# A two-layer hybrid mixer: gates and a product moved ahead of the recurrence's levels, and two roots taken as powers

## The chip, the core and the metric

The kernel runs on one core of one Trainium2 chip, in one launch. Its time is the device time of a run, in microseconds; three runs of the kernel before gave 2448.23, 2448.4 and 2450.8, a median of 2448.4. TensorE is called PE here, VectorE DVE, ScalarE ACT, GpSimd POOL, and SyncE (which issues the loads of the weights) SP.

## The reference

The program is two blocks one behind the other on 256 positions of width 1024. The change is in the second, in its hybrid mixer, once in each of two layers. From one projection `h @ w_in` a layer makes three mixers and joins them in one output product:

```python
proj = h @ w_in                               # qa ka va | qd kd vd | qh fh ih gh
z     = q_a @ k_a.T / 8                       # stick-breaking, 4 heads of 64, causal
log_w = log_sigmoid(z) + tail                 # tail: sum of log_sigmoid(-z) to the right
o_a   = exp(log_w) @ v_a
o_d   = dilated_mixture(rope(rms(qd)), rope(rms(kd)), vd)
log_f = logaddexp(log(lb), log1p(-lb) + log_sigmoid(fh))   # recurrence, 4 heads of 128
scores[t, s] = sum_d q_h[t, d] * k_h[s, d] * exp(g[t, d] - g[s, d])   # g = cumsum(log_f), s <= t
o_h   = rms(scores @ ih (+ the state of earlier chunks)) * gain * silu(gh)
y     = concat(o_a, o_d, o_h) @ w_out
x     = x + g2 * y
```

Everything is float32.

## The kernel before

A product with a weight matrix is three matmuls in a rounded format, hi*hi, lo*hi and hi*lo (`mm3`, L135 to L139). The weights come in 1 MB slots (128 x 2048, `load`); `split_w` (L113 to L131) cuts a slot into four pieces, for each of which ACT writes the high half (L125) and DVE the low half (L128), out of a pool of eight pieces each. `dense_A` makes 128 rows x 512 columns of a product, `dense_B` the transposed form. Results go to PSUM tiles of two tags with four buffers each, `w` and `acc`.

One layer of `hybrid` goes through these steps, in the order of the program before:

1. Products for the dilated attention, its roots (`rsqrt` at site 'd', L1185), rotation (L1186 to L1200), transposes (L1206), scores (L1219), softmax, transposes (L1243) and output (L1251).
2. Products for the recurrence: queries (L1263), forget gates (L1268), logarithm (L1273), running sums `G` by a scan on DVE (L1278).
3. Products `qa`, `ka`, `va` of the stick-breaking mixer (L1284 to L1288).
4. The recurrence's scores: the diagonal (L1300, L1304), then seven levels n = 0 to 6 (L1305 to L1335). A level takes differences of `G` on POOL (L1317, L1318), the exponential on ACT (L1319), two multiplications on DVE (L1320, L1321), eight matmuls with 64 columns on PE (L1328) and a masked copy into `ST` on DVE (L1331). The tile `E` of a level has three buffers, so level n + 3 waits for the matmuls of level n.
5. Stick-breaking: scores z (L1346, L1350), scaled by six operations on DVE (L1354 to L1356); Abs, Exp, Ln on ACT (L1358 to L1360) and their sum on DVE (L1361); tails on PE (L1366 to L1370); the weights' exponential (L1372); output (L1379, L1382).
6. The output gates: product 3072 with Sigmoid (L1393) and two multiplications (L1394, L1396); then the recurrence's values, product 2560 (`ih`, L1401).
7. The recurrence's output, half by half t = 0, 1: matmuls (L1421, L1422), Square (L1427), sum (L1429), root (`rsqrt` at site 'o', L1430), two multiplications (L1431, L1432), transposes (L1435), copies into `yT`.
8. The gate row (L1083) and the output product `y @ w_out` in four quarters: halves of the inner dimension (k0 = 0, 4) by halves of the columns (n = 0, 1); the quarters with k0 = 0 need only the two attention mixers.

The program is not run in this order. A scheduler of the language puts the instructions of each engine in an order when the kernel is built, by its own estimate of times and by the place in the program; on the chip each engine takes its instructions in that fixed order and waits where an input isn't there. So a step that is moved in the text changes the order of many others.

`root` (L171 to L189) forms a power -1/2. At the sites named in `PW` it is one POOL instruction with `ALU.pow` (L175); at the others it is a Newton iteration of twelve small operations on DVE (L179 to L188).

Of the kernel before, what the change touches and what calls it, by code (L numbers as in the profile page):

```python
# [11 lines left out]
F32 = mybir.dt.float32  # L12
# [8 lines left out]
P = 128  # L21
D = 1024
S = 256
# [17 lines left out]
def kernel(ctx: ExitStack, tc: tile.TileContext, A: dict, out: bass.AP, phases=None):  # L41
# [128 lines left out]
    PW = 'bqvwt'  # L170
# [979 lines left out]
    def hybrid(l, tables):  # L1150
# [3 lines left out]
        with tc.tile_pool(name=f"hyb{l}", bufs=1, reuse_waits="tile") as wk:  # L1154
# [134 lines left out]

            ST = t4("ST")  # L1290
# [45 lines left out]
            def parts6(v):  # L1336
                return v[:, :1024].rearrange("p (h t) -> p h t", h=4), v[:, 1024:].rearrange("p (h t) -> p h t", h=4)

            zm = m6()
            z0, z1 = parts6(zm)  # L1340
            p0 = [ps("acc").rearrange("p (i t) -> p i t", i=2) for _ in range(2)]
            p1 = [ps("acc")[:, :S].rearrange("p (i t) -> p i t", i=2) for _ in range(2)]
            for i in range(2):
                for j in range(2):
                    r = slice(64 * j, 64 * j + 64)
                    PE.matmul(p0[j][:, i], ka[r, i, :P], qa[r, i], start=True, stop=True, skip_group_check=True)  # L1346
            for i in range(2):
                for j in range(2):
                    r = slice(64 * j, 64 * j + 64)
                    PE.matmul(p1[j][:, i], ka[r, i, P:], qa[r, i, P:], start=True, stop=True, skip_group_check=True)  # L1350
            neg = sbneg[:, None, :].to_broadcast([P, 2, P])
            for j in range(2):
                hs = slice(2 * j, 2 * j + 2)
                V.scalar_tensor_tensor(z0[:, hs, :P], p0[j][:, :, :P], 0.125, neg, ALU.mult, ALU.add)  # L1354
                V.tensor_scalar(z0[:, hs, P:], p0[j][:, :, P:], 0.125, None, ALU.mult)
                V.scalar_tensor_tensor(z1[:, hs], p1[j], 0.125, neg, ALU.mult, ALU.add)  # L1356
            sp = m6()
            ACT.activation(sp, zm, AF.Abs)  # L1358
            ACT.activation(sp, sp, AF.Exp, scale=-1.0)
            ACT.activation(sp, sp, AF.Ln, bias=1.0)  # L1360
            V.scalar_tensor_tensor(sp, zm, 0.0, sp, ALU.max, ALU.add)  # L1361
            s0, s1 = parts6(sp)
            for b in range(2):
                pt = ps("acc").rearrange("p (i t) -> p i t", i=2)
                hs = slice(2 * b, 2 * b + 2)
                PE.matmul(pt, tri, s0[:, hs], start=True, stop=False, skip_group_check=True)  # L1366
                PE.matmul(pt[:, :, P:], ones, s1[:, hs], start=False, stop=True, skip_group_check=True)
                V.tensor_tensor(z0[:, hs], z0[:, hs], pt, ALU.subtract)
            pt = ps("acc")
            PE.matmul(pt, tri, sp[:, 1024:], start=True, stop=True)  # L1370
            V.tensor_tensor(zm[:, 1024:], zm[:, 1024:], pt, ALU.subtract)
            ACT.activation(zm, zm, AF.Exp)  # L1372
            pt = ps("acc").rearrange("p (i t) -> p i t", i=2)
            for i in range(2):
                for j in range(2):
                    r = slice(64 * j, 64 * j + 64)
                    hd = 2 * i + j
                    vs = slice(64 * hd, 64 * hd + 64)
                    PE.matmul(  # L1379
                        pt[r, i], va[:, 0, vs], z0[:, 2 * j + i], start=i == 0, stop=False, skip_group_check=True  # L1380
                    )
                    PE.matmul(  # L1382
                        pt[r, i, P:], va[:, 1, vs], z1[:, 2 * j + i], start=False, stop=True, skip_group_check=True
                    )
            for i in range(2):
                put_T(yT[0][:, i], yT[1][:, i], pt[:, i])

            mod_cols(l, 2)
            gh = t4("h4", bufs=3).rearrange("p a b -> p (a b)").rearrange("p (t n) -> p t n", t=2)
            g128 = bcast_row(wk, A["hgrn_norm_g_2"][l], P, "g128")  # L1390
            po = dense_A(h, w, 3072, 512)
            for t in range(2):
                ACT.activation(gh[:, t], po[t], AF.Sigmoid)  # L1393
                V.tensor_tensor(gh[:, t], gh[:, t], po[t], ALU.mult)  # L1394
                ghv = gh[:, t].rearrange("p (h v) -> p h v", h=4)
                V.tensor_tensor(ghv, ghv, g128[:, None, :].to_broadcast([P, 4, P]), ALU.mult)  # L1396
# [45 lines left out]
            for k0 in (0, 4):  # L1442
                for n in range(2):
                    dense_A(yT, A["w_out_2"][l], 512 * n, 512, k0, 4, po[2 * n : 2 * n + 2], (0, 7))
                    if k0 == 4:
                        for t in range(2):
                            add_gated(wk, po[2 * n + t], g, t, n)
# [188 lines left out]
```

## Time and profile before

| | |
|---|---|
| median of three runs | 2448.4 us |
| the profiled execution, its own time | 2449.72 us |
| its span in the profile | 2447.9 us |
| busy: PE, DVE, ACT, POOL | 88%, 50%, 40%, 13% |
| loads by SP's queue | 715.70 MB, 74.9% of the 16 engines' time |
| mean granted clock of PE | 0.927 |

The span is cut in 40 slices of 61 us each on the page. The first mixer of the change lies from 1531 to 1688 us, in slices 26 to 28; the second from 2088 to 2245 us, in slices 35 to 37. A granted clock of 1.00 is PE's upper level (2.4 GHz), 0.50 the lower (1.2 GHz).

### The profile page before, as it was taken

To read this page: it belongs to the slowest core of one execution; us is meant where nothing else is said; L and a number is where in the kernel's file an instruction comes from. 1 tells how busy PE (TensorE), PEld (TensorE's weight loads), DVE (VectorE), ACT (ScalarE), POOL (GpSimd) and SP (SyncE) were. 2 spreads that over 40 slices of the span, in tenths; PEclk is the share of its full clock that TensorE was granted. 3 is DMA by queue.
4 is the path that set the end of the run, shared out by engine and by line. 5 is a ranking of instruction groups with operands and counts; after the bars stand their busy time and mean duration, and the time that the engine had idled before them with its cause. 6 is when DMAs were issued, how large, how long until landed. Compare 5 with 4: busy or idle time off the path is not lost.

```text
span 2447.9 us, 38767 instructions
## 1 busy us (share of the span) xinstructions
PE 2147.4 (88%) x15680; PEld 1591.2 (65%) x15680; DVE 1230.1 (50%) x2277; ACT 979.2 (40%) x1834; POOL 315.3 (13%) x198
## 2 busy tenths in 40 slices
PE   8998867787689987677666999989999999999999
PEld 7887424443257843222113999877998999887998
DVE  6765101000048631000003996878986986878655
ACT  6653110000036510000003774656765775557553
POOL 2000000000000000000000650031640550030100
PEclk9999979888889998878778999999999999989999
DMA  7377999999983899999997885625875785624652
GB/s 301 128 301 318 418 420 419 420 420 420 420 339 104 327 383 419 419 420 420 420 420 299 326 302 193 222 69 187 320 278 185 288 308 195 221 87 146 234 188 87
DMA packets 100211, 721.35 MB, mean 295 GB/s; under 512 B 11470, under 2 KB 11598, under 8 KB 12992
## 3 DMA queue, kind: packets, MB, share of 16 engines
q1 hardware_dynamic: 98640, 715.70, 74.9%
q0 software_dynamic: 1104, 3.06, 0.5%
q8 instruction: 123, 2.02, 0.3%
q14 instruction: 56, 0.46, 0.0%
q10 hardware_dynamic: 288, 0.12, 0.0%
HBM read 717.78 MB, written 1.05 MB: 294 GB/s over the span
## 4 chain that ended last, share of the span: by engine, by line
PE 59%; DMA 31%; DVE 5%; ACT 2%; issue 2%; POOL 0%; SPq 0%; DVEq 0%; POOLq 0%; ACTq 0%
PE w L139 12%; PE w L138 12%; PE w L137 12%; DMA slot<-in_w_down_dram 9%; DMA slot<-in_w_up_dram 8%; DMA slot<-in_w_gate_dram 8%; DMA slot<-in_xattn_w_kv_dram 4%; PE acc L137 3%; PE acc L138 3%; PE acc L139 3%; PE w L958 2%; PE w L819 1%; PE w L993 1%; PE acc L1328 1%; PE acc L434 1%
## 5 line engine op out<-in xcount | busy, mean ns | idle before, releaser
L128 DVE TENSOR_TENSOR wl<-slot,wh 128x512 fp32r<-128x512 f32 x854 | 695.8, 844 | 222.4 <-ACT wh L125 218.4
L125 ACT ACTIVATE wh<-slot 128x512 fp32r<-128x512 f32 x856 | 522.7, 627 | 311.9 <-PE w L139 165.7
L137 PE MATMUL w<-hTh,wh 128*128 128x256 f32 x1792 | 511.6, 286 | 8.1 <-ACT hTh L356 6.1
L138 PE MATMUL w<-hTh,wl 128*128 128x256 f32 x1792 | 511.1, 285 | 3.2 <-DVE wl L128 3.2
L139 PE MATMUL w<-hTl,wh 128*128 128x256 f32 x1792 | 511.3, 285 | 0.0
L958 PE MATMUL w<-slot,XgT 128*32 128x256 f32 x4096 | 316.6, 445 | 126.6 <-DMA slot<-in_w_up_dram 93.7
L137 PEld LDWEIGHTS w<-hTh,wh 128*128 128x128 f32 x1792 | 346.4, 193 | 13.1 <-ACT hTh L356 7.0
L138 PEld LDWEIGHTS w<-hTh,wl 128*128 128x128 f32 x1792 | 346.1, 193 | 7.0 <-DVE wl L128 4.4
L139 PEld LDWEIGHTS w<-hTl,wh 128*128 128x128 f32 x1792 | 346.1, 193 | 4.5 <-issue 3.3
L958 PEld LDWEIGHTS w<-slot,XgT 128*32 128x32 f32 x4096 | 126.7, 122 | 312.8 <-DMA slot<-in_w_up_dram 154.9
L982 DVE TENSOR_TENSOR a<-a,w 128x256 f32<-128x256 f32 x32 | 13.5, 420 | 513.3 <-ACT a L982 513.3
L982 ACT ACTIVATE a<-w 128x256 f32<-128x256 f32 x32 | 12.3, 384 | 484.7 <-PE w L958 467.4
L993 PE MATMUL w<-slot,aT 128*32 128x512 f32 x1024 | 154.5, 689 | 51.7 <-DMA slot<-in_w_down_dram 33.1
L459 POOL TENSOR_TENSOR mprod<-mprod 128x1024 f32<-128x1024 f32 x44 | 124.8, 2835 | 173.2 <-ACT mprod L458 144.9
L137 PE MATMUL acc<-wh,ah 128*128 128x512 f32 x352 | 138.5, 393 | 0.0
L138 PE MATMUL acc<-wh,al 128*128 128x512 f32 x352 | 137.3, 390 | 0.0
L139 PE MATMUL acc<-wl,ah 128*128 128x512 f32 x352 | 137.1, 390 | 0.0
L458 ACT ACTIVATE mprod<-slot,cm 128x512 f32<-128x512 f32 x176 | 120.3, 711 | 23.8 <-DMA slot<-in_w_mod_dram 23.7
L993 PEld LDWEIGHTS w<-slot,aT 128*32 128x32 f32 x1024 | 29.5, 117 | 152.0 <-DMA slot<-in_w_down_dram 82.4
L137 PE MATMUL w<-wh,hTh 128*128 128x512 f32 (+1 forms) x320 | 118.7, 372 | 9.5 <-DVE hTl L267 7.0
L139 PE MATMUL w<-wl,hTh 128*128 128x512 f32 (+1 forms) x320 | 118.1, 373 | 0.0
L138 PE MATMUL w<-wh,hTl 128*128 128x512 f32 (+1 forms) x320 | 117.4, 368 | 0.1
(404 smaller groups left out, 2689.0 us busy)
## 6 DMA issues: line engine op xcount, KB each, us to landing
slot<-in_w_gate_dram SPq DMA_DIRECT2D x128, 1024.0 KB, 19.9
slot<-in_w_up_dram SPq DMA_DIRECT2D x128, 1024.0 KB, 19.9
slot<-in_w_down_dram SPq DMA_DIRECT2D x128, 1024.0 KB, 19.9
slot<-in_w_mod_dram SPq DMA_DIRECT2D x72, 1024.0 KB, 5.1
slot<-in_ffn_w_gate_dram SPq DMA_DIRECT2D x44, 1024.0 KB, 5.1
slot<-in_ffn_w_up_dram SPq DMA_DIRECT2D x44, 1024.0 KB, 5.1
slot<-in_ffn_w_down_dram SPq DMA_DIRECT2D x44, 1024.0 KB, 5.0
slot<-in_w_in_dram SPq DMA_DIRECT2D x42, 1024.0 KB, 5.8
```

Source lines behind the costliest of these rows:

```text
L125: lead["act"] = ACT.activation(hi, r[:, c], AF.Copy)
L128: low = eng[i].tensor_tensor(lo, r[:, c], hi.bitcast(F32), ALU.subtract)
L137: PE.matmul(o, a[0], b[0], start=start, stop=False, skip_group_check=True)
L138: PE.matmul(o, a[1], b[0], start=False, stop=False, skip_group_check=True)
L139: lead["pe"] = PE.matmul(o, a[0], b[1], start=False, stop=stop, skip_group_check=True)
L434: PE.matmul(mod_now["pm"][CAP * i : CAP * i + CAP], cm[:, ka + i, 31 - j : 63 - j], raw[:, i], start=first, stop=True, skip_group_check=Tr ...
L458: ACT.activation(f[:, i], raw[:, i], AF.Copy, scale=cm[:, ka + i, 31:32])
L459: POOL.tensor_tensor(f[:, :2], f[:, :2], f[:, 2:], ALU.add)
L819: PE.matmul(po[:, b], a, m, start=k == 0 and b == 0, stop=k == KC - 1, skip_group_check=True)
L958: PE.matmul(gu[CAP * g : CAP * g + CAP, 256 * wi : 256 * wi + 256], XgT[:, e // 4 % 2, k, e % 4 * CAP : e % 4 * CAP + CAP], raw[:, kk, 256 ...
L982: past = [ACT.activation(a, gu[:, :256], AF.Silu), V.tensor_tensor(a, a, gu[:, 256:], ALU.mult)]
L993: PE.matmul(py[CAP * g : CAP * g + CAP], aT[:, j, CAP * i : CAP * i + CAP], raw, start=i == 0, stop=i == 3, skip_group_check=True, tile_po ...
```

## The change

The order of steps 3 to 8 is another. The product 2560 (`ih`) now stands behind `va`; then come the stick-breaking mixer and the gates with product 3072 and the gate row; only then the recurrence's diagonal and its seven levels. The quarter (n = 0, k0 = 0) of the output product stands behind level 3, the quarter (n = 1, k0 = 0) behind the recurrence's output, and the quarters with k0 = 4 come in the order n = 0, 1 as before. The gates and the gate row go into buffers of the stick-breaking mixer (`m6`, two buffers) and no longer into `h4`. The Sigmoid of the gates is queued behind the exponential of the weights (`weights_done`). The roots at sites 'o' and 'd' become powers on POOL. The loads on SP's queue stand in the same order as before.

```diff
-    PW = 'bqvwt'
+    PW = 'bqvwtod'
...
             for t in range(2):
                 ACT.copy(va[:, t], po[t][:, :256])
 
-            ST = t4("ST")
...
+            ih = wk.tile([P, 2, 512], F32, name=uid("ih"))
+            po = dense_A(h, w, 2560, 512)
+            for t in range(2):
+                ACT.copy(ih[:, t], po[t])
+
             def parts6(v):
...
-            ACT.activation(zm, zm, AF.Exp)
+            weights_done = ACT.activation(zm, zm, AF.Exp)
...
-            gh = t4("h4", bufs=3).rearrange("p a b -> p (a b)").rearrange("p (t n) -> p t n", t=2)
+            gh = m6()[:, :1024].rearrange("p (t n) -> p t n", t=2)
...
-                ACT.activation(gh[:, t], po[t], AF.Sigmoid)
+                with queued([weights_done]):
+                    ACT.activation(gh[:, t], po[t], AF.Sigmoid)
...
-            ih = wk.tile([P, 2, 512], F32, name=uid("ih"))
-            po = dense_A(h, w, 2560, 512)
-            for t in range(2):
-                ACT.copy(ih[:, t], po[t])
-
+            g = m6()[:, :1024]
+            gate_row(g, ms, 5, 1.0)
+            po = []
+
+            def out_half(n, k0):
+                if not k0:
+                    po.extend(ps("w") for _ in range(2))
+                dense_A(yT, A["w_out_2"][l], 512 * n, 512, k0, 4, po[2 * n : 2 * n + 2], (0, 7))
+
+            ST = t4("ST")
...
+                if n == 3:
+                    out_half(0, 0)
             X = t4("h4", bufs=3)
...
-            g = t4("h4", bufs=3).rearrange("p a b -> p (a b)")
-            gate_row(g, ms, 5, 1.0)
-            po = [ps("w") for _ in range(4)]
-            for k0 in (0, 4):
-                for n in range(2):
-                    dense_A(yT, A["w_out_2"][l], 512 * n, 512, k0, 4, po[2 * n : 2 * n + 2], (0, 7))
-                    if k0 == 4:
-                        for t in range(2):
-                            add_gated(wk, po[2 * n + t], g, t, n)
+            out_half(1, 0)
+            for n in range(2):
+                out_half(n, 4)
+                for t in range(2):
+                    add_gated(wk, po[2 * n + t], g, t, n)
```

The moved code is the same in its new place, with other line numbers: L1346 and L1350 are L1305 and L1309 after, L1361 is L1320, L1366 is L1325, L1300 is L1377, L1328 is L1405, L1422 is L1434, L1435 is L1447.

How the engines' orders change is shown at three places, in the first layer. The first is PE around the transposes of the rotated queries and keys. `w_11457` is the first half of the recurrence's queries (48 matmuls) and `w_11526` the second half in the order before; after, they are `w_11445` and `w_11514`. Before:

```order
L137 MATMUL w_11526<-hTh_11052,wh_11537 128x256
L138 MATMUL w_11526<-hTh_11052,wl_11538 128x256
L1206 MATMUL acc_11355<-cst,m_1982_11339 128x128
L1206 MATMUL acc_11361<-cst,m_1982_11339 128x128
L139 MATMUL w_11526<-hTl_11053,wh_11537 128x256
```

After:

```order
L138 MATMUL w_11445<-hTh_11052,wl_11457 128x256
L139 MATMUL w_11445<-hTl_11053,wh_11456 128x256
L1206 MATMUL acc_11343<-cst,m_1981_11327 128x128
L1206 MATMUL acc_11349<-cst,m_1981_11327 128x128
L137 MATMUL w_11445<-hTh_11052,wh_11460 128x256
L138 MATMUL w_11445<-hTh_11052,wl_11461 128x256
```

The first transposes stood behind 77 matmuls of the two halves (rows 3777 and 3778 of PE's order), and stand behind 36 (rows 3736 and 3737).

The second place is DVE between the levels and the sum of the stick-breaking mixer. `acc_12087` to `acc_12090` before, and `acc_12038` to `acc_12041` after, are the scores z. Before, behind the last level's masked copies:

```order
L1331 COPY_PREDICATED ST_11960<-masks,acc_12076 128x512
L128 TENSOR_TENSOR wl_12251<-slot_12240,wh_12250 128x512
L1354 SCALAR_TENSOR_TENSOR m_2097_12086<-acc_12087,late 128x2x128
L1355 TENSOR_SCALAR m_2097_12086<-acc_12087 128x2x128
L1356 SCALAR_TENSOR_TENSOR m_2097_12086<-acc_12089,late 128x256
```

After (`h_2141` and `h_2143` are the tiles E of levels 1 and 2, `slot_12098` and `slot_12140` hold the weights of product 3072):

```order
L1398 TENSOR_TENSOR h_2141_12225<-h_2141_12225,qh_11443 128x16x32
L1397 TENSOR_TENSOR h_2143_12241<-h_2143_12241,kh_11442 128x32x16
L128 TENSOR_TENSOR wl_12109<-slot_12098,wh_12108 128x512
L1398 TENSOR_TENSOR h_2143_12241<-h_2143_12241,qh_11443 128x32x16
L128 TENSOR_TENSOR wl_12113<-slot_12098,wh_12112 128x512
L128 TENSOR_TENSOR wl_12143<-slot_12140,wh_12142 128x512
L128 TENSOR_TENSOR wl_12147<-slot_12140,wh_12146 128x512
L128 TENSOR_TENSOR wl_12151<-slot_12140,wh_12150 128x512
L128 TENSOR_TENSOR wl_12155<-slot_12140,wh_12154 128x512
L1313 SCALAR_TENSOR_TENSOR m_2100_12037<-acc_12038,late 128x2x128
L1314 TENSOR_SCALAR m_2100_12037<-acc_12038 128x2x128
```

The scaling of z no longer stands behind the levels; it stands behind the multiplications of levels 0 to 2 and the eight splits of product 3072. On PE that product comes behind the scores z, and 35 of its 48 matmuls stand ahead of the tails (L1325 after); the other 13 stand behind them.

The third place is PE in the recurrence's output. `acc_12339` before and `acc_12378` after is the output of half t = 0, `o_12383` its tile behind the root and the gate. Before:

```order
L1411 MATMUL acc_12332<-h_2151_12326 128x128 x4
L1422 MATMUL acc_12339<-ih_12237,ST_11960 128x128 x4
L1083 MATMUL w_12422<-ms_78,cst 128x512
L1083 MATMUL w_12425<-ms_78,cst 128x512
L137 MATMUL w_12428<-wh_12434,yTh_11172 128x512
```

After:

```order
L1423 MATMUL acc_12371<-h_2164_12365 128x128 x4
L1434 MATMUL acc_12378<-ih_11948,ST_12195 128x128 x4
L138 MATMUL w_12437<-wh_12448,yTl_11173 128x512
L139 MATMUL w_12437<-wl_12449,yTh_11172 128x512
L137 MATMUL w_12437<-wh_12452,yTh_11172 128x512
L138 MATMUL w_12437<-wh_12452,yTl_11173 128x512
L139 MATMUL w_12437<-wl_12453,yTh_11172 128x512
L1447 MATMUL acc_12392<-cst,o_12383 128x128 x4
L1433 MATMUL acc_12405<-ih_11948,S_2166_12376 128x128
```

Before, the two matmuls of the gate row and 17 matmuls of the output product stand between half 0 and its transposes (L1435); after, five matmuls of the output product do. Between half 1 and its transposes there were 31 matmuls of the output product, and there are 15. In the same order after, the matmuls of levels 0, 1 and 2 follow each other with nothing between them, and the 16 first matmuls of the quarter (0, 0) stand between levels 2 and 3.

## Rows read from the trace of the kernel before

**Rows 1.** The page: the span.

```profile
span 2447.9 us, 38767 instructions
```

**Rows 2.** Windows, first layer: stretch and us, busy time by engine, granted clock, DMA.

```profile
1608.30:1612.70 4.40, 0.03 (x1) 0.06 (x1) 3.08 (x3) 2.11 (x2) 4.40 (x5) 1.00 0.52 210
1613.10:1623.20 10.10, 10.10 (x44) 9.62 (x44) 5.57 (x7) 3.77 (x5) 5.69 (x5) 0.50 0.01 2
1637.70:1651.30 13.60, 12.38 (x55) 9.67 (x53) 8.42 (x15) 11.71 (x13) 0.00 (x0) 1.00 0.22 78
```

**Rows 3.** Windows: levels of the second layer; idle stretches and what follows them.

```profile
2169.50:2183.00 13.50, 13.50 (x54) 12.44 (x54) 7.61 (x10) 4.89 (x6) 7.72 (x6) 0.50 0.00 1
1893.40:1895.00 1.60, 0.08 (x2) 0.04 (x1) 1.12 (x3) 0.97 (x3) 0.00 (x0) 1.00 0.69 287
1896.40:1899.70 3.30, 3.30 (x18) 3.30 (x17) 2.94 (x8) 2.61 (x6) 0.00 (x0) 0.50 0.68 286
2250.90:2255.80 4.90, 3.42 (x25) 3.16 (x26) 4.51 (x12) 3.29 (x8) 0.00 (x0) 1.00 0.96 393
```

**Rows 4.** Timeline of PE: levels 0 and 4: start, us, operation, idle before, releaser.

```profile
1612.67 3.30 PE L1328 MATMUL acc<-h 128*128 128x64 f32 x16 [4.40 <-DVE h L1321]
...
1628.18 1.92 PE L1328 MATMUL acc<-h 128*128 128x64 f32 x16
```

**Rows 5.** Groups on PE, end of the output product: busy us, mean ns.

```profile
L137 PE MATMUL w<-wh,yTh 128*128 128x512 f32 x16 | 6.3, 395 | 0.0
```

**Rows 6.** Timeline of DVE: root 'd' and the rotation, first layer.

```profile
1554.57 0.17 DVE L193 TENSOR_SCALAR ms<-rq 128x16 f32<-128x16 f32 x1
...
1560.53 1.22 DVE L1186 TENSOR_TENSOR m<-m,rq 128x1024 f32<-128x1024 f32 x1
...
1565.15 0.42 DVE L1200 TENSOR_TENSOR m<-m,h 128x256 f32<-128x256 f32 x1
```

**Rows 7.** Source line of the power on POOL: ns min, median, max, first and last start.

```profile
L175 POOL TENSOR_TENSOR rms<-ss,half x16: 538/562/993, 332.6 to 2248.7; 128x1 f32<-128x1 f32 x16
L175 POOL TENSOR_TENSOR rq<-ms,half x2: 3534/3534/3534, 46.7 to 739.6; 128x20 f32<-128x20 f32 x2
```

**Rows 8.** Timeline of POOL and ACT: level 0.

```profile
1604.38 3.11 POOL L1317 TENSOR_TENSOR h<-G 128x512 f32<-128x512 f32 x1 [67.50 <-DVE G L1278]
1607.45 1.05 POOL L1318 TENSOR_TENSOR h<-G 128x512 f32<-128x512 f32 x1
...
1608.53 1.06 ACT L1319 ACTIVATE h<-h 128x1024 f32<-128x1024 f32 x1 [2.23 <-POOL h L1318]
```

**Rows 9.** Timeline of DVE: multiplications of levels 0 and 6, a split, scaling of z.

```profile
1609.62 1.46 DVE L1320 TENSOR_TENSOR h<-h,kh 128x512 f32<-128x512 f32 x1 [1.77 <-ACT h L1319]
...
1632.42 0.68 DVE L1321 TENSOR_TENSOR h<-h,qh 128x512 f32<-128x512 f32 x1
...
1633.09 0.68 DVE L128 TENSOR_TENSOR wl<-slot,wh 128x512 fp32r<-128x512 f32 x1
...
1637.52 0.40 DVE L1354 SCALAR_TENSOR_TENSOR m<-acc,late 128x256 f32<-128x256 f32 x1
```

**Rows 10.** Timeline of ACT and DVE: logarithm and sum of the stick-breaking mixer.

```profile
1645.96 0.61 ACT L125 ACTIVATE wh<-slot 128x512 fp32r<-128x512 f32 x1
1646.59 1.28 ACT L1360 ACT_TABLE_LOAD   x1
1647.89 1.49 ACT L1360 ACTIVATE m<-m 128x1536 f32<-128x1536 f32 x1
...
1649.41 1.76 DVE L1361 SCALAR_TENSOR_TENSOR m<-m,m 128x1536 f32<-128x1536 f32 x1 [2.11 <-ACT m L1360]
```

**Rows 11.** Timeline of ACT and DVE: recurrence's output, half 0.

```profile
1661.77 0.60 ACT L1427 ACTIVATE o<-acc 128x512 f32<-128x512 f32 x1 [0.91 <-PE acc L1422]
...
1662.45 0.68 DVE L1429 TENSOR_REDUCE ro<-o 128x4 f32<-128x512 f32 x1
...
1666.41 0.69 DVE L1432 TENSOR_TENSOR o<-o,h 128x512 f32<-128x512 f32 x1
```

More of the change, by code (lines that the diff above doesn't have):

```diff
@@ new lines, in hybrid @@
+            p1 = [ps("acc")[:, :S].rearrange("p (i t) -> p i t", i=2) for _ in range(2)]
+            for i in range(2):
+                for j in range(2):
+                    r = slice(64 * j, 64 * j + 64)
+                    PE.matmul(p0[j][:, i], ka[r, i, :P], qa[r, i], start=True, stop=True, skip_group_check=True)
+            for i in range(2):
+                for j in range(2):
+                    r = slice(64 * j, 64 * j + 64)
+                    PE.matmul(p1[j][:, i], ka[r, i, P:], qa[r, i, P:], start=True, stop=True, skip_group_check=True)
@@ new lines, in hybrid @@
+            neg = sbneg[:, None, :].to_broadcast([P, 2, P])
+            for j in range(2):
+                hs = slice(2 * j, 2 * j + 2)
+                V.scalar_tensor_tensor(z0[:, hs, :P], p0[j][:, :, :P], 0.125, neg, ALU.mult, ALU.add)
+                V.tensor_scalar(z0[:, hs, P:], p0[j][:, :, P:], 0.125, None, ALU.mult)
+                V.scalar_tensor_tensor(z1[:, hs], p1[j], 0.125, neg, ALU.mult, ALU.add)
+            sp = m6()
+            ACT.activation(sp, zm, AF.Abs)
+            ACT.activation(sp, sp, AF.Exp, scale=-1.0)
@@ new lines, in hybrid @@
+            ACT.activation(sp, sp, AF.Ln, bias=1.0)
+            V.scalar_tensor_tensor(sp, zm, 0.0, sp, ALU.max, ALU.add)
+            s0, s1 = parts6(sp)
+            for b in range(2):
+                pt = ps("acc").rearrange("p (i t) -> p i t", i=2)
+                hs = slice(2 * b, 2 * b + 2)
+                PE.matmul(pt, tri, s0[:, hs], start=True, stop=False, skip_group_check=True)
+                PE.matmul(pt[:, :, P:], ones, s1[:, hs], start=False, stop=True, skip_group_check=True)
+                V.tensor_tensor(z0[:, hs], z0[:, hs], pt, ALU.subtract)
@@ new lines, in hybrid @@
+            pt = ps("acc")
+            PE.matmul(pt, tri, sp[:, 1024:], start=True, stop=True)
+            V.tensor_tensor(zm[:, 1024:], zm[:, 1024:], pt, ALU.subtract)
+            weights_done = ACT.activation(zm, zm, AF.Exp)
+            pt = ps("acc").rearrange("p (i t) -> p i t", i=2)
+            for i in range(2):
+                for j in range(2):
+                    r = slice(64 * j, 64 * j + 64)
+                    hd = 2 * i + j
+                    vs = slice(64 * hd, 64 * hd + 64)
+                    PE.matmul(
+                        pt[r, i], va[:, 0, vs], z0[:, 2 * j + i], start=i == 0, stop=False, skip_group_check=True
+                    )
+                    PE.matmul(
+                        pt[r, i, P:], va[:, 1, vs], z1[:, 2 * j + i], start=False, stop=True, skip_group_check=True
+                    )
@@ L1335, in hybrid @@
                 )
[L1336 to L1368, printed above, removed]
@@ L1369, in hybrid @@
-            pt = ps("acc")
-            PE.matmul(pt, tri, sp[:, 1024:], start=True, stop=True)
-            V.tensor_tensor(zm[:, 1024:], zm[:, 1024:], pt, ALU.subtract)
-            ACT.activation(zm, zm, AF.Exp)
[L1373 to L1384, printed above, removed]
```

23 lines of the change are left out of this document (14 added, 9 removed).

## The prediction

> **What bounds the kernel now.** I read the page first, then cut the first mixer into windows by what PE does, then read the timelines of the engines that PE waits for, and last the orders. In the mixers PE sets the end: up to the levels its matmuls follow each other, so what a change here is worth is what PE doesn't do at its full pace from there on. Full pace I take from the end of the output product: three groups of 16 matmuls in 11.0 us between 1677.2 and 1688.4, 0.229 us for a matmul of 512 columns, although each is shown with 395 ns because they overlap [rows 5]. From the start of the recurrence's diagonal at 1604.0 to the end of the output product at 1688.4 I find three losses.
>
> A. At level 0 PE waits 4.4 us for DVE [rows 2, 4]: differences on POOL 3.11 and 1.05 us, the exponential 1.06 [rows 8], two multiplications of 1.46 beside POOL [rows 9]. Layer two has the same stretch.
>
> B. Behind that wait the granted clock is 0.50 for 10.1 us in layer one and 13.5 in layer two [rows 2, 3], while PE always has work: a level takes 3.30 us at the lower clock and 1.92 at the upper [rows 4]. At the upper clock the same work would need half: 5.1 and 6.8 us lost.
>
> C. From 1637.7 to 1651.3, beside the stick-breaking chain, 52 of the 55 matmuls are products; at 0.229 they would need 11.9 us of 13.6 [rows 2]. The next 30 go at about that pace too, another 1.0 by estimate. Together 2.7.
>
> Sum that could be won: 12.2 us in layer one, 13.9 in layer two.
>
> **The change part by part.** The number of products, levels and loads stays, and SP's order with it; the loads have room, DMA is busy 0.22 in the window of C [rows 2]. What changes is who waits.
>
> Moving the levels behind the gates removes A: POOL, ACT and DVE can prepare levels 0 to 2 while PE makes products, three tiles E being there. With A goes the cause of B, and C is left out of the old place. I count -12.2 and -13.9 and add what is late instead.
>
> D, root 'd' as a power. The power on POOL takes 0.562 us for one column and 3.534 for twenty [rows 7]: (3.534 - 0.562) / 19 = 0.156 a column, 2.9 us for the 16 columns here and 1.03 for the four of root 'o'. The Newton root's input is ready at 1554.74 and its user L1186 starts at 1560.53; the power lets L1186 start at about 1557.8, and the first rotated rows are there 5.04 us later, as before (1560.53 to 1565.57) [rows 6]: 1562.8. But in the new order PE comes to the transposes 41 matmuls of 256 columns earlier, at half of 0.229 each 4.7 us: at 1560.8, if it took them as they came at 1565.5 before. So PE waits 2.0 us; behind it stand all products of the recurrence. Bounds: 0 if 16 columns cost hardly more than one, 3.0 if they cost as much as twenty (3.53) and start late.
>
> The Trainium skill (GPSIMD Engine Reference, section 3.1) gives about 2.6 cycles an element for an elementwise operation on this engine, next to DVE's one. By that the 16 columns would cost a few hundredths of a microsecond more than one column, D would be gone and the sum 2.0 us a layer lower. The trace disagrees for a power [rows 7], and I go by the trace.
>
> E, the stick-breaking sum. Its scores z now stand behind product 2560 on PE, and their scaling on DVE behind levels 0 to 2 and eight splits. I count from the end of the running sums G, which I put 3.3 us ahead of the end of product `va` on PE (an estimate: D moves PE back by 2, and the chain to G comes nearly 2 sooner because the second softmax is ordered further ahead; before, they end together). PE: 3.3, then 48 x 0.229 = 11.0 for product 2560, 2.1 for z, 0.4 for transposes and 35 x 0.229 = 8.0 of product 3072: out of work at 24.8. DVE: 4.2 and 1.1 for level 0 on POOL and ACT [rows 8], 2 x 1.46 beside POOL, four splits at 0.6, four multiplications at 0.68, eight splits at 0.6, six scalings at 0.34 from start to start [rows 9]: 20.2 with the hand-overs, 3.8 us after PE has made z. Then Abs, Exp and Ln on the same 1536 columns, 1.49 each, two splits' halves of 0.6 between them, one table load of 1.28 and the sum 1.76 [rows 10], 8.7 in all: 28.9. PE waits 4.1 us for the tails. Queued behind them on PE are 13 products, the whole of the gate row, levels and output. Bounds: 0.3 if DVE scales z as soon as PE has made it, 6 if POOL slows DVE's splits too.
>
> The table load counts 1.28 us here since the function behind it starts 0.02 after its end [rows 10]. The Trainium skill (ScalarE: Activation LUTs, What ACT_TABLE_LOAD costs) gives 1.28 us for the load and adds 1.38 for draining the engine. By the page E would be 1.4 longer, the sum 2.8 higher over both layers. No row here shows the drain.
>
> F, the recurrence's output. From the matmuls of half 0 to its transposes stand Square 0.60, sum 0.68, a split 0.6, scale 0.17, power 1.03, two multiplications of 0.69 and hand-overs of 0.3: 4.8 us (from 1661.77 to 1667.10 it was 5.3 with the Newton root) [rows 11]. Before, PE had 17 products and the gate row to do meanwhile, and waited for nothing; now it has five products, 1.1 us. Wait 3.6. For half 1 the chain is 4.5 and 15 products give 3.4: wait 1.1. Together 4.7; bounds 3 and 6. In the levels themselves DVE is ready 0 to 3 us before PE by the same counting, so I add nothing there, and take up to 1 a layer into the range.
>
> At the upper clock: D + E + F = 2.0 + 4.1 + 4.7 = 10.8 added, 12.2 and 13.9 removed: -1.4 and -3.1.
>
> G, the clock behind the new waits. The idle 4.4 us were followed by 0.50 in both layers; of two idle stretches of 1.5 us elsewhere one was followed by 3.3 us at 0.50, and the other by none: PE is busy 3.4 of 4.9 us there, all at 1.00 [rows 3]. Half of 3.3 is 1.7 lost. For the waits E and F (4.1 and 3.6) I take 1.4 each, since part of the slow stretch falls into the wait, and for D 1.2: 4.0 a layer. Bounds: 0, and 10 if two of them hold as long as B did.
>
> Sum: -1.4 - 3.1 + 2 x 4.0 = +3.5 us. On the profiled execution's own 2449.7 (its span of 2447.9 [rows 1] and 1.8 around it) that is 2453.2; it stood 1.3 above the median, so 2448.4 + 3.5 = 2451.9 for the median of runs. I say 2452.
>
> **The rivals.** R1, faster: the clock holds. If PE gets past the new waits without leaving the upper clock, G is 0 and the time 2448.4 - 4.5 = 2443.9; if DVE also scales z 2 us sooner than I count in each layer, 2440. For it speaks that the waits are shorter than A and dense products follow E at once; against it, that an idle 1.5 us was enough once [rows 3].
>
> R2, clearly slower: the lower clock reaches the levels. Levels 0, 1 and 2 now follow each other with no product between them, about 10 us behind wait E, the length for which the clock stayed down in B. At the lower clock they cost 3.30 instead of 1.92 each [rows 4], 4.1 more, and the diagonal, taken as one more level by estimate, 1.4: 5.5 a layer, 2452 + 11 = 2463. It decides from the point where the clock is still 0.50 when the diagonal starts. Against it: level 4 of layer one had a single product ahead of it and ran at the upper clock (1.92).
>
> R3, the change does not do what it says: no product fills levels 0 to 2, only 16 matmuls stand ahead of level 3, so A comes back at a later level because E of level 3 waits for level 0's matmuls (POOL 2.1, exponential 1.06, multiplications 2 x 0.68 to 1.46 [rows 8, 9]). My count puts it 1 us ahead of PE; if it is late by 2 us, the time is 2452 + 4 = 2456.
>
> **How the numbers follow.** Less than 0.2%, 4.9 us, can't be told from no change. The forecast (new waits take the place of the old, 2446 to 2458) gets 0.50, R1 0.25, R2 0.15, R3 0.10. Of the forecast 0.35 lies within 4.9 us of before, 0.13 above and 0.02 below; of R1 0.24 is faster and 0.01 the same; R2 is slower; of R3 0.06 is slower and 0.04 the same. Sums: faster 0.26, same 0.40, slower 0.34. The range reaches from R1 with a shorter E to R2: 2440 to 2463.
>
> **What would show it.** In the profile after: an idle PE of about 2 us ahead of the first transposes L1206, released by DVE; a row of the power with 128x16 near 2.9 us and one with 128x4 near 1.0; idle PE of about 4 us ahead of L1325 and of 3 to 4 ahead of the first L1447; no wait of 4.4 us at level 0; windows at 0.50 of some 3 us behind these waits. I am wrong if PE does not wait at L1325 (then E, and the time is near R1), if the power of 16 columns takes under 1 us (D), or if the levels run at 3.3 us (R2).

## The result, and the profile after

The changed kernel took 2464.26 us (median of four runs, 2462.71 to 2466.18); the kernel before took 2448.32 beside it (2445.37 to 2450.8). The ratio is 1.0063, with a 95% interval of 1.0051 to 1.0076: clearly slower, by 15.9 us. The forecast was 3.5 us slower, 2452, in a range up to 2463. By the prediction's own measure (4.9 us can't be told from no change) that was "the same", which had 0.40; slower had 0.34. So the measured time lies above the range, and the size of the loss was not forecast.

The waits that the prediction named are all there. These are PE's rows in the first mixer after (start us, us, operation, in brackets the idle time before and what ended it), to be held against [rows 4]:

```profile
1548.05 0.50 PE L139 MATMUL w<-wl,hTh 128*128 128x512 f32 x1 [1.21 <-DVE wl L128]
...
1565.18 0.44 PE L1206 MATMUL acc<-cst,m 128*128 128x128 f32 x2 [2.67 <-DVE m L1200]
...
1635.56 1.19 PE L1325 MATMUL acc<-m,late 128*128 128x512 f32 x1 [4.27 <-issue]
...
1646.06 0.44 PE L1338 MATMUL acc<-m,va 128*64 128x256 f32 x2 [1.23 <-ACT m L1331]
...
1651.17 5.47 PE L1405 MATMUL acc<-h 128*128 128x64 f32 x48
...
1681.25 0.63 PE L1447 MATMUL acc<-cst,o 128*128 128x128 f32 x4 [3.93 <-DVE o L1444]
...
1689.60 0.63 PE L1447 MATMUL acc<-cst,o 128*128 128x128 f32 x4 [0.86 <-DVE o L1444]
```

Level 0 doesn't wait any more: 48 matmul records of levels 0 to 2 go in one stretch of 5.47 us. The 4.27 us are put down to "issue"; the inputs tell more: the sum that L1325 reads starts on DVE at 1633.70 and takes 1.76, so the wait ended with DVE's work (in the second layer the wait is put down to that sum, L1320, itself). The windows after (stretch and us, busy time of PE, PEld, DVE, ACT, POOL, granted clock, DMA), against [rows 2]:

```profile
1565.72:1569.13 3.41, 3.41 (x19) 3.41 (x18) 3.41 (x9) 1.05 (x1) 0.00 (x0) 0.50 0.00 0
...
1633.99:1640.82 6.83, 5.26 (x9) 2.83 (x10) 3.36 (x4) 0.71 (x2) 0.00 (x0) 0.50 0.43 149
...
1649.40:1674.20 24.80, 24.55 (x173) 22.18 (x171) 23.64 (x31) 11.99 (x18) 10.99 (x8) 1.00 0.13 43
...
1681.78:1685.19 3.41, 3.41 (x18) 3.41 (x18) 0.88 (x3) 0.83 (x3) 0.00 (x0) 0.50 0.35 147
```

At each of the three long waits a stretch at the granted clock 0.50 begins, the second one 1.6 us before its wait ends; in the levels, 1649.4 to 1674.2, it is 1.00, and DVE is busy 23.64 of 24.80 us there.

The power on POOL, to be held against [rows 7], has 16 columns once and four columns for each half:

```profile
1556.76 3.29 POOL L175 TENSOR_TENSOR rq<-ms,half 128x16 f32<-128x16 f32 x1 [19.47 <-DVE ms L193]
...
1678.27 1.39 POOL L175 TENSOR_TENSOR ro<-ms,half 128x4 f32<-128x4 f32 x1 [12.73 <-DVE ms L193]
...
1686.99 1.01 POOL L175 TENSOR_TENSOR ro<-ms,half 128x4 f32<-128x4 f32 x1 [7.34 <-DVE ms L193]
```

The start of the mixer on ACT, and what stands ahead of the tails on DVE and ACT, to be held against [rows 9, 10]:

```profile
1543.00 0.63 ACT L125 ACTIVATE wh<-slot 128x512 fp32r<-128x512 f32 x1 [1.24 <-DMA slot<-in_w_in_dram]
...
1606.67 5.67 DVE L128 TENSOR_TENSOR wl<-slot,wh 128x512 fp32r<-128x512 f32 x4
1612.26 1.52 DVE L1397 TENSOR_TENSOR h<-h,kh 128x512 f32<-128x512 f32 x1
1613.71 1.60 DVE L1398 TENSOR_TENSOR h<-h,qh 128x512 f32<-128x512 f32 x1
1615.23 2.48 DVE L128 TENSOR_TENSOR wl<-slot,wh 128x512 fp32r<-128x512 f32 x4
...
1626.97 1.49 ACT L1317 ACTIVATE m<-m 128x1536 f32<-128x1536 f32 x1 [4.81 <-DVE m L1315]
```

ACT's first split waits 1.24 us for its weights. Four splits on DVE take 5.67 us beside POOL's differences and 2.48 without them. PE has made z at 1622.75; ACT gets it, scaled by DVE, at 1626.97.

The account of one layer, PE from the transposes of its input to those of the next (idle times from PE's rows; the clock is half of the time at 0.50 in which PE was not waiting), in us:

| term | predicted, layer 1 / 2 | measured |
|---|---|---|
| A, wait at level 0 | -4.4 / -4.4 | -4.40 / -4.40 |
| B, clock behind A | -5.1 / -6.8 | -5.1 / -6.8 |
| C, slow feeding | -2.7 / -2.7 | 0 / 0 (1.22 before, 1.23 after) |
| D, ahead of L1206 | 2.0 | 2.67 / 2.67 |
| E, ahead of L1325 | 4.1 | 4.27 / 4.23 |
| F, ahead of the two L1447 | 4.7 | 4.79 / 4.71 |
| G, clock behind D, E, F | 4.0 | 6.0 / 4.9 |
| a wait for a weight load, ahead of L139 | not seen | 1.21 / 0.53 |
| sum | 2.6 / 0.9 | 9.4 / 5.8 |

15.2 us together; the two kernels' medians differ by 15.9. The lengths of the two mixers say the same without any terms. The windows over them are 156.1 and 157.2 us long before, and 165.1 and 163.2 after, 15.0 more:

```profile
1537.00:1693.10 156.10, 149.59 (x954) 127.56 (x952) 127.91 (x263) 94.88 (x158) 20.50 (x16) 0.97 0.43 149
2092.90:2250.10 157.20, 150.89 (x953) 128.88 (x951) 127.97 (x263) 94.85 (x158) 20.51 (x16) 0.96 0.42 148
...
1537.60:1702.70 165.10, 150.42 (x952) 126.71 (x952) 127.22 (x227) 95.72 (x160) 26.59 (x19) 0.96 0.40 141
2102.60:2265.80 163.20, 149.30 (x953) 126.04 (x952) 127.15 (x227) 95.72 (x160) 26.59 (x19) 0.97 0.40 142
```

### The profile page after: what moved, and what is told of

It is laid out like the page before. It is cut to its first block, busy times and chain, and to the rows that moved or that the text cites. A ratio compares the mean times of both kernels' runs of the same rounds, so it can differ in the third digit from the quotient of the medians.

```text
span 2464.3 us, 38710 instructions
## 1 busy us (share of the span) xinstructions
PE 2145.8 (87%) x15680; PEld 1591.1 (65%) x15680; DVE 1227.0 (50%) x2205; ACT 982.7 (40%) x1838; POOL 325.3 (13%) x204
## 4 chain that ended last, share of the span: by engine, by line
PE 57%; DMA 34%; DVE 5%; ACT 2%; issue 1%; POOL 1%; SPq 0%; DVEq 0%; ACTq 0%; POOLq 0%
PE w L138 12%; PE w L139 12%; PE w L137 12%; DMA slot<-in_w_up_dram 12%; DMA slot<-in_w_down_dram 11%; DMA slot<-in_w_gate_dram 9%; PE acc L137 3%; PE acc L138 3%; PE acc L139 3%; PE w L958 1%; PE acc L1405 1%; DVE wl L128 1%; PE acc L434 1%; PE w L993 1%; DMA slot<-in_w_in_dram 1%
## 5 line engine op out<-in xcount | busy, mean ns | idle before, releaser
L128 DVE TENSOR_TENSOR wl<-slot,wh 128x512 fp32r<-128x512 f32 x854 | 703.4, 854 | 226.3 <-ACT wh L125 222.4
L139 PE MATMUL w<-hTl,wh 128*128 128x256 f32 x1792 | 512.7, 286 | 0.0
L958 PE MATMUL w<-slot,XgT 128*32 128x256 f32 x4096 | 311.2, 439 | 127.8 <-DMA slot<-in_w_up_dram 98.0
L139 PEld LDWEIGHTS w<-hTl,wh 128*128 128x128 f32 x1792 | 348.0, 194 | 3.6 <-issue 2.3
L139 PE MATMUL acc<-wl,ah 128*128 128x512 f32 x352 | 137.1, 390 | 0.0
L139 PE MATMUL w<-wl,hTh 128*128 128x512 f32 (+1 forms) x320 | 116.2, 366 | 1.7 <-DVE wl L128 1.7
L1012 ACT COPY y<-w 128x512 f32<-128x512 f32 x30 | 17.6, 586 | 249.4 <-PE w L993 249.4
```

What stands on the lines that cost most here:

```text
L128: low = eng[i].tensor_tensor(lo, r[:, c], hi.bitcast(F32), ALU.subtract)
L139: lead["pe"] = PE.matmul(o, a[0], b[1], start=False, stop=stop, skip_group_check=True)
L958: PE.matmul(gu[CAP * g : CAP * g + CAP, 256 * wi : 256 * wi + 256], XgT[:, e // 4 % 2, k, e % 4 * CAP : e % 4 * CAP + CAP], raw[:, kk, 256 ...
```

## The experiments

Each was run beside the kernel before, and the ratios are to its runs in the same session. "Cover" is the products that PE has to do while another engine works on what PE needs next. The "softplus chain" is Abs, Exp and Ln on ACT and the sum on DVE, from the scaled z to the tails.

**1. Root 'd' alone undone.** Edit: `PW = 'bqvwto'`.

> The changed kernel with the Newton root at site 'd' again; all moves stay. Theory 1 (wait D is caused by the power's place in PE's order: the builder puts the transposes 41 matmuls earlier than the power delivers): PE's order at the transposes is that of before, the wait of 2.67 us ahead of L1206 and the 3.4 us at the lower clock behind it go in both layers, 2 x (2.67 + 1.7) = 8.7 us, about 2455. Rival (the power does shorten the chain, and the wait has another cause, a DVE that is late from the start of the mixer): the root takes longer, the wait stays or grows by 2 us a layer, 2464 to 2468.

2459.01 us, 1.0040 (1.0027 to 1.0054). The wait at L1206 and the lower clock behind it went, as theory 1 has it. The gain was smaller, 5 to 6 us and not 8.7, because PE came sooner to the tails and waited longer there:

```profile
1629.32 2.04 PE L1325 MATMUL acc<-m,late 128*128 128x512 f32 x2 [6.14 <-issue]
```

Of the 2.67 us of D 1.87 went into E.

**2. Root 'o' alone undone.** Edit: `PW = 'bqvwtd'`.

> The changed kernel with the Newton root at site 'o' again; 'd' stays a power, all moves stay. Theory 1 (the wait ahead of L1447 is the length of the chain behind the matmuls of a half, with too few products to cover it): the root costs DVE 12 small operations instead of 1.0 to 1.4 us on POOL, 5.3 instead of 4.8 us of chain, so the two waits grow by 0.5 to 1 us each, 2 x 1 to 2 = 2 to 4 us slower, 2466 to 2468. Rival (POOL's power is the wait): the waits shrink by 1 us each, 2460.

2469.12 us, 1.0082 (1.0068 to 1.0096): slower than the change, as theory 1 has it, by somewhat more than it said. The wait at half 0 is 5.18 us, 1.25 longer than with the power. The wait at half 1 did not grow (0.70 us); in its place came two short ones behind it, 0.37 us ahead of the next product and 0.62 ahead of the next transposes. So this part of the change helped, by about as much as root 'd' cost.

**3. Product 2560 behind z.**

```diff
-            po = dense_A(h, w, 2560, 512)
...
                 V.scalar_tensor_tensor(z1[:, hs], p1[j], 0.125, neg, ALU.mult, ALU.add)
+            ih = wk.tile([P, 2, 512], F32, name=uid("ih"))
+            po = dense_A(h, w, 2560, 512)
+            for t in range(2):
+                ACT.copy(ih[:, t], po[t])
+
             sp = m6()
```

> The changed kernel with product 2560 behind the scores z instead of ahead of them. Theory 1 (wait E is a matter of the cover: 35 matmuls behind z against a chain of 8.7 us that starts late): 48 matmuls stand behind z, DVE scales z ahead of the splits of product 3072, the wait of 4.27 us shrinks to 1 us or less and the window at the lower clock behind it goes, 2 x (3.3 + 2 to 3) = 11 to 13 us faster, about 2452. Rival (DVE is simply full in this stretch, and the wait comes back at the next place, ahead of the output of the stick-breaking mixer L1338, which then has 9 products of cover instead of 13): 2460 to 2464.

2460.02 us, 1.0045 (1.0033 to 1.0058). The time is the rival's, but the waits are not where either theory has them: the wait ahead of the tails is 4.72 us with 48 products of cover, and none stands at L1338. What was gained is that wait of 1.23 us and 0.9 at the first L1447 (3.05). The trace shows why the tails still wait: z is made at 1612.4 and not scaled before 1617.6.

```profile
1607.22 5.66 DVE L128 TENSOR_TENSOR wl<-slot,wh 128x512 fp32r<-128x512 f32 x4
1612.81 1.53 DVE L1397 TENSOR_TENSOR h<-h,kh 128x512 f32<-128x512 f32 x1
...
1617.59 0.41 DVE L1308 SCALAR_TENSOR_TENSOR m<-acc,late 128x256 f32<-128x256 f32 x1
```

DVE is at splits that POOL's differences make 2.3 times as long, and at level 0's multiplications. That gave the next theory.

**4. The levels' differences held behind z's scaling.**

```diff
+            hold = wk.tile([P, 1], F32, name=uid("hold"))
+            held = POOL.tensor_copy(hold, z1[:, 3, P - 1 : P])
...
+                with queued([held]):
+                    LV[0].tensor_tensor(El, ref, Gl, ALU.subtract)
+                    LV[1].tensor_tensor(Eu, Gu, ref, ALU.subtract)
```

> The changed kernel; POOL's differences of all levels wait for the scaling of z (a copy of one column of z on POOL, and the differences queued behind it). Theory 1 (wait E comes from the levels' preparation: beside POOL's differences of levels 0 to 2 four splits on DVE take 5.66 us instead of 2.4 and two multiplications 3.1 instead of 1.4, all ahead of z's scaling): z is scaled about 2 us sooner against PE, 39 products instead of 35 stand ahead of the tails, the wait of 4.27 us falls to 1 to 2 us and its window at the lower clock shrinks: 2 x (3 + 1.5) = 9 us faster, about 2455. Rival (DVE is behind in any case, and the levels' preparation then comes late for level 0): the wait moves to L1405, 2462 to 2468.

2454.99 us, 1.0027 (1.0016 to 1.0037): 9 us faster than the change, the time of theory 1. The way there is partly another: the wait ahead of the tails fell to 3.12 us and not to 1 to 2, but the wait of 1.23 us at L1338 went with it, and in neither layer is the clock at 0.50 behind the tails' wait. Eight splits now take less than four did:

```profile
1606.50 4.92 DVE L128 TENSOR_TENSOR wl<-slot,wh 128x512 fp32r<-128x512 f32 x8
...
1635.14 1.10 PE L1327 MATMUL acc<-m,late 128*128 128x512 f32 x2 [3.12 <-issue]
```

**5. The quarter (1, 0) held behind half 0.** Edit: `with queued([half0]): out_half(1, 0)`, where `half0` is the last matmul of half 0.

> The changed kernel; the output quarter (n = 1, k0 = 0) is queued on PE behind the matmuls of half 0, so 14 products instead of 5 stand ahead of the transposes of half 0, 23 instead of 15 ahead of those of half 1, and 19 fewer among the levels. Theory 1 (wait F is a matter of where the cover was spent: the levels are bound by PE and DVE alike, and products there are taken from F): the wait of 3.93 us falls to 2, the second goes, the lower clock behind it too, and the levels lose little: 2 x (2 + 0.9 + 1.7) = 9 us faster, 2455. Rival (DVE, busy 23.6 of 24.8 us in the levels, sets their pace, so PE stands idle there for the 19 products that were taken out): 4.4 us a layer come back as idle time ahead of L1405, the sum is near nothing, 2462 to 2466.

2466.72 us, 1.0072 (1.0060 to 1.0085). The rival was right, with a time just above its range. F fell to 0.89 and 0.72, and two waits for DVE came up in the levels and behind them:

```profile
1669.57 2.31 PE L1405 MATMUL acc<-h 128*128 128x64 f32 x16 [1.99 <-DVE h L1398]
1673.87 2.05 PE L1423 MATMUL acc<-h 128*128 128x128 f32 x8 [1.99 <-DVE h L1419]
```

So in this stretch DVE sets the pace: the 3.2 us that F lost came back as 4.0 us of waits in and just behind the levels.

**6. The roots alone, nothing moved.** Edit, to the kernel before: `PW = 'bqvwtod'`.

> The kernel before with both roots as powers and no move. Theory 1 (D is the power's place in PE's order, whatever stands behind): a wait of 2.7 us ahead of L1206 and 3.4 us at the lower clock behind it in each layer, no wait at L1435 since 17 and 31 products stand there: 2 x (2.7 + 1.7) = 8.8 us slower, 2458. Rival (the later waits swallow it: level 0's wait of 4.4 us is for DVE and POOL, whose chain the power makes shorter): 2449 to 2452.

2449.72 us, 1.0000 (0.9991 to 1.0008). The rival was right. D is there, 2.69 us ahead of L1206, but level 0's wait of 4.40 shrank to 1.81:

```profile
1609.18 3.19 PE L1328 MATMUL acc<-h 128*128 128x64 f32 x22 [1.81 <-DVE h L1321]
```

Here the PE that was held up early waited less at the next place: 2.69 and 1.81 us add up to 4.50, against the 4.40 of before. The lower clock behind level 0 did not shrink with the wait: 10.2 and 13.7 us, as before. Without the moves the two roots together cost nothing. With them root 'd' costs 5 us (run 1) and root 'o' gains 5 (run 2), so, if these two add up, the pair is not what made the change slow.

**7. Both remedies together.** Edits of 1 and 4.

> The changed kernel with the Newton root at 'd' and POOL's differences of the levels behind the scaling of z, the two edits that each alone gave 5.3 and 9.3 us. Theory 1 (D and E are separate waits): they add up, 2464.3 - 5.3 - 9.3 = 2449.7, with no wait at L1206 and 3 us ahead of the tails. Rival (without D the chain to the tails is later against PE, as in the run without 'd' alone, where the wait there grew from 4.27 to 6.14 us): the wait at the tails grows to 5 us and the lower clock returns behind it, 2453 to 2456.

2448.35 us, 1.0000 (0.9991 to 1.0009). Theory 1: they add up, and the whole loss is gone. The tails wait 3.12 us, the recurrence's output still 3.59.

**8. And product 2560 behind z.** Edits of 1, 3 and 4.

> The same, and product 2560 behind the scores z. Theory 1 (what is left of E is cover): 48 products, 11.0 us, stand between z and the tails, against 2.1 us of scaling and 8.5 of softplus chain, so PE waits 0 to 1 us there; ahead of the output of the stick-breaking mixer 11 products, 2.5 us, stand against 4 us of chain, a wait of 1.5; the recurrence's output still waits 3.5 to 4: 2443 to 2447, the changed order then just better than before. Rival (the levels' differences, now beside the splits of product 3072, slow DVE there and the wait comes back at the levels): 2450 to 2455.

2452.70 us, 1.0013 (1.0005 to 1.0022), slower than without. The wait at the tails fell to 1.82 and 3.16 us came up at the next place, the output of the stick-breaking mixer, with 11 products of cover. The rival has the time, but the wait it expected at the levels is only 0.49 us; the place is the one of theory 1, with twice its wait.

**9. The load of g128 later.** Edit to the change: its `bcast_row` stands in `queued` behind the power 'd'.

> The changed kernel; POOL's load of the gain g128 (64 KB in small packets) is issued behind the power 'd' instead of 1 us ahead of the first weight loads of the mixer. Theory 1 (the new waits of 1.21 and 0.53 us at 9.2 us into each mixer, PE behind ACT's first split behind a weight load, come from that load's place): the load of the weights lands 1 to 2 us sooner, the wait goes, 2 x 1 = 1 to 2 us faster, 2462.5. Rival (the weight loads are late because of the slots, not of that load): the wait stays, 2464.

2461.78 us, 1.0054 (1.0042 to 1.0067). The idle times of 1.21 and 0.53 us are gone in both layers, as theory 1 has it. The 2.5 us between the medians are within the two intervals.

**10. Edits of 1, 4 and 9 together** (the load of g128 behind the copy `held`).

> The changed kernel with the Newton root at 'd', POOL's differences of the levels behind the scaling of z, and the load of g128 behind the same point on POOL. Theory 1 (the three losses are separate): 2448.35 - 2.5 = 2445.9, with no idle PE at 9.2 us into the mixers, some 3 us ahead of the tails and 3.6 us at the recurrence's output left. Rival (the first wait only moves: the sooner start is lost again ahead of the tails): 2448 to 2449, the wait there 1 us longer.

2449.34 us, 1.0000 (0.9990 to 1.0009): not faster than without the third. The rival has the time. The early wait is gone; the tails wait 3.27 and 3.66 us, 0.15 and 0.40 more than in run 7, and the second wait of the recurrence's output grew from 0.41 and 0.45 to 0.89 and 0.88.

**11. Product 2560 ahead of the levels, alone.** Edit to the kernel before: the four lines of `ih` moved ahead of `ST = t4("ST")`.

> The kernel before, with one edit: product 2560 ahead of the recurrence's levels. Theory 1 (A and B are recoverable by any 11 us of products at level 0): the wait of 4.4 us at level 0 and the stretch at the lower clock go, 9.5 and 11.2 us; the stick-breaking chain loses 48 products of cover: 32 products and the gate row, 8.6 us, stand behind z against a chain of 11 to 12, and nothing ahead of the output L1384, so 3 + 4 us of new waits and some 2 us of clock a layer come back: 2445, between 2440 and 2450. Rival 1 (the clock falls behind any of these waits and stays down): 2455. Rival 2 (the chain is covered after all, since DVE and ACT have less to do there): 2430.

2447.89 us, 0.9993 (0.9984 to 1.0002), within theory 1's range and not to be told from no change. The new waits, the first of which theory 1 did not have:

```profile
1619.77 2.63 PE L1333 MATMUL acc<-h 128*128 128x64 f32 x16 [1.14 <-DVE ST L1309]
...
1648.97 1.10 PE L1371 MATMUL acc<-m,late 128*128 128x512 f32 x2 [2.54 <-issue]
...
1655.40 1.13 PE L1384 MATMUL acc<-m,va 128*64 128x256 f32 x4 [2.75 <-ACT m L1377]
```

**12 and 13. z ahead of the levels; z behind level 3.** Both on top of 11: the lines from z's matmuls to the softplus sum moved.

> The kernel before; the scores z, their softplus chain and product 2560 stand ahead of the recurrence's levels, the tails and the weights behind the levels, gates and outputs as before, Newton roots. Theory 1 (what counts is which chain runs beside which products: A, B recoverable by 11 us of products, the softplus chain by products and levels, the recurrence's output by 24 to 30 products): A and B go as in the run with product 2560 alone (9.5 and 11.2 us a layer), and the waits of 2.5 and 2.75 us ahead of the tails and the output of the stick-breaking mixer that came up there too: 2449 - 20 + 4 = 2433, between 2428 and 2440. Rival (ACT and DVE can't run both chains side by side: POOL's differences slow DVE, the tables change on ACT, and level 0 is late again): 2445 to 2450.

> The kernel before with product 2560 ahead of the levels and the scores z with their softplus chain behind level 3 instead of behind level 6; gates and outputs as before, Newton roots. Theory 1 (each chain needs its own cover: 11 us of products at level 0; 27 products and three levels beside the softplus chain; 14 products and the gate row ahead of the output L1385; 37 and 24 products at the recurrence's output): the waits of 2.5 and 2.75 us that the run with product 2560 alone had go, and the clock behind them: 2448 - 10 = 2438, between 2433 and 2443. Rival (DVE is full in the levels, and what the softplus chain takes there comes back as waits ahead of levels 4 to 6): 2446 to 2452.

2464.42 us, 1.0059 (1.0047 to 1.0071), and 2451.88, 1.0015 (1.0006 to 1.0023): both theories 1 wrong. The rival of 13 has its time, the rival of 12 is 14 us short. In 12, rows of PE and of DVE:

```profile
1629.67 3.65 PE L1359 MATMUL acc<-h 128*128 128x64 f32 x16 [8.27 <-DVE ST L1335]
...
1622.33 6.55 DVE L128 TENSOR_TENSOR wl<-slot,wh 128x512 fp32r<-128x512 f32 x6
1628.81 1.32 DVE L1335 COPY_PREDICATED ST<-masks,acc 128x512 f32<-128x512 uint8 x2
```

The masked copies, which free PE's accumulators, stand on DVE behind the softplus sum and the splits of product 3072. The 1.14 us at level 0 in 11 and the 1.15 in 13 end with the same copies; the longest wait of 13, 2.03 us at a level, ends with the scaling of z on DVE, which frees accumulators too.

**14, 15, 16. The splits of product 3072 behind a masked copy.** On top of 11. In 14 they stand behind level 2's copy; in 15 and 16 behind level 0's, and z behind level 4 or 5:

```diff
-                V.copy_predicated(
+                copied = V.copy_predicated(
...
+                if n == 0:
+                    held = copied
+                if n == 5:
...
+                    zm = m6()
...
-            po = dense_A(h, w, 3072, 512)
+            with queued([held]):
+                po = dense_A(h, w, 3072, 512)
```

> The kernel before with product 2560 ahead of the levels (as in the run with that alone) and DVE's splits of product 3072 behind the masked copy of level 2. Theory 1 (the wait at level 0 there is the order of eight splits ahead of the copies that free PE's accumulators): no wait at the levels, no lower clock behind it, 38 products instead of 32 between z and the tails, 6 ahead of the output of the stick-breaking mixer: 1.14 + 2 to 3 + 1 to 2 a layer, 2448 - 10 = 2438, between 2434 and 2442. Rival (DVE's work in the levels is what it is, and the copies wait elsewhere): 2446 to 2449.

> Product 2560 ahead of the levels, splits of product 3072 behind the masked copy of level 0, and the scores z behind level 4 instead of 6. Theory 1 (the softplus chain then runs beside two levels and 26 products, and no wait is left but small ones): 2434 to 2440. Rival (as in the run with z behind level 3: the scaling of z on DVE and the exponential stand in the levels' way, 2 us of wait there and the lower clock behind it): 2445 to 2452.

> The same with z behind level 5: one level and 26 products beside the softplus chain, 7 products ahead of the output of the stick-breaking mixer. Theory 1: less in the way of the levels, less cover for the chain: 2436 to 2441, 1 to 2 us of wait left in the stick-breaking mixer. Rival: 2445 to 2450, as above.

2445.17 us, 0.9984 (0.9975 to 0.9993); 2442.50, 0.9973 (0.9962 to 0.9983); 2438.59, 0.9956 (0.9943 to 0.9969). The last is 11 us faster than before and 26 faster than the change. 14 lies between its two theories: the wait for the diagonal's copies went, but PE waits 2.46 us for DVE at a later level. 15 lies between its two as well; 16 is within theory 1. In 16 the granted clock is 1.00 throughout in both mixers. First the windows of its two mixers, then the largest waits of PE that are left in the first:

```profile
1536.70:1688.60 151.90, 145.89 (x953) 122.94 (x952) 127.68 (x263) 94.31 (x158) 21.25 (x16) 1.00 0.44 153
2087.10:2239.00 151.90, 145.87 (x953) 122.94 (x951) 127.82 (x263) 94.30 (x158) 21.27 (x16) 1.00 0.44 153
```

```profile
1625.91 1.97 PE L1333 MATMUL acc<-h 128*128 128x64 f32 x16 [1.24 <-DVE h L1326]
1635.44 1.97 PE L1333 MATMUL acc<-h 128*128 128x64 f32 x16 [0.69 <-DVE m L1363]
1646.60 1.10 PE L1374 MATMUL acc<-m,late 128*128 128x512 f32 x2 [1.30 <-issue]
1652.58 0.66 PE L1387 MATMUL acc<-m,va 128*64 128x256 f32 x4 [0.69 <-ACT m L1380]
```

The same stretches take 156.1 and 157.2 us before, 9.5 more together. Little of this is waiting: PE is not busy for 6.5 and 6.3 us there before and for 6.0 and 6.0 in run 16. The rest, 8.7 us, is the same matmuls in less busy time, at 1.00 in place of 0.97 and 0.96. Run 15 has the same 1.24 us ahead of a level, and there 6.8 us at 0.50 follow. So most of what run 16 gained is that the clock stayed up, and why it did is not shown.

## Why the prediction was wrong

A and B held: the wait at level 0 and the slow stretch behind it are gone. The forecast's picture, new waits in the place of the old, is the one that came; what failed are the sizes of its terms. D, E and F held in place and nearly in size (2.67 for 2.0, 4.25 for 4.1, 4.75 for 4.7, as means of the layers), R1 fell because PE waited at all three, R3 because no level waited more than 0.3 us, and R2 because the levels ran at the clock of 1.00.

The step that failed most is the term C, counted as 2 x 2.7 us won with nothing in its place. It was read from a window's mean, and the 1.0 of it for "the next 30" was guessed. The rows of before show products at the full pace of 0.23 us and one single wait:

```profile
1649.94 0.50 PE L137 MATMUL w<-wh,hTh 128*128 128x512 f32 x1 [1.22 <-ACT wh L125]
```

That wait, 1.22 us and not 2.7, is for ACT, which is in the stick-breaking chain. After, a wait of the same size for the same chain, 1.23 us, stands ahead of L1338, where the prediction had none. Nothing was won: this is 5.4 us of the 11.7 by which the sum (15.2) is over the forecast (3.5).

The second is G, 8.0 for 10.9: at each of the six long waits there was a window at 0.50, of 3.4 to 6.8 us. D was 1.3 short (0.4 a layer is the power, 3.29 us for 2.9; the other 0.3 are not traced to one row, and the late weights are not in it, since run 9 has 2.67 without them), and the weight load's wait, 1.7 in both layers, was missed: SP's order was looked at, but not where POOL's load of g128 stands to it.

E came out right in size, in part by luck. The count had level 0's multiplications wait for POOL and ACT, 5.3 us behind the running sums G. In the trace POOL's two differences take 2.55 us there and not 4.2, and the multiplications start 6.1 us behind G because four splits stand ahead of them (there are sixteen behind G in all, the count had twelve), at 1.42 us each beside POOL's differences and not 0.6. The 20.2 of the prediction "with the hand-overs" is the bare sum of its parts; there is nothing for hand-overs in it. With the differences held back (run 4) E is 3.12 and the slow stretch behind it is gone. That E and D are not additive (run 1) was not in the working; nor was it needed for the sum.

The range failed by 1.3 us because its upper end was R2 alone. The upper bounds written beside D, E, F and G together allowed some 20 us above the forecast, and no case held several of them.

The power took 3.29 us for 16 columns, against 0.56 for one [rows 7]. By the 2.6 cycles an element that the Trainium skill (GPSIMD Engine Reference, section 3.1) gives, the 15 columns more would by estimate cost a few hundredths of a microsecond; the trace disagrees, and the prediction was right to go by the trace. The drain that the Trainium skill (ScalarE: Activation LUTs, What ACT_TABLE_LOAD costs) adds to a table load is not in this trace either: the load starts at 1630.89, 0.03 us behind the split ahead of it, takes 1.28 us, and the Ln starts at 1632.18.

What the runs show of the cause is this: with root 'd' undone and the differences held back (run 7) the whole loss is gone, so it comes and goes with D and with what makes E late. That C was nothing is read from the traces and was not tested by a run. What stays open is why the same wait is followed by the lower clock in one run and not in another (below).

## What to carry to other kernels

A wait at one place is not a sum to be won. Products that cover it are taken from another chain, and here the stick-breaking chain and the recurrence's output lost what level 0 gained. Before moving work ahead, read what will stand in each in-order queue in front of the next operation that PE waits for; the best version came from moving less (one product, and z by one level) and from holding eight splits behind the copies that free accumulators, and most of its gain is a clock that stayed up, for which the runs show no cause. Read a stretch's loss from the rows in it, not from the mean of a window.

## What was not expected of the hardware

- DVE's splits beside POOL's differences take 1.42 us each and 0.62 without (5.67 for four, 4.92 for eight).
- The clock behind a wait is not a function of the wait. A wait of 2.69 us ahead of L1206 in run 6 is followed by no window at 0.50 in the first layer and by one of 6.8 us in the second; 1.24 us ahead of a level are followed by 6.8 us at 0.50 in both layers of run 15, and by none in run 16. Level 0's wait of 4.40 us before and of 1.81 in run 6 are both followed by 10.2 us in the first layer and 13.7 in the second.
- The same power of four columns took 1.39 us at half 0 and 1.01 at half 1. DVE runs a split beside the first and nothing beside the second; no run tests whether that is the cause.
